# A hybrid decoder layer: sparse results stored as two halves, keys evacuated by whole tiles, one transpose for two heads' compressed probabilities

## The chip, the cores and the metric

The kernel runs on one core of a Trainium2 chip. A core has TensorE (PE in the profile; its weight loads are listed apart as PEld), VectorE (DVE), ScalarE (ACT), GpSimd (POOL) and SyncE (SP), which here issues all transfers of the kernel's data. The metric is the device time in microseconds of one execution; the median of three runs is compared.

## The reference

One layer on x of 1024 tokens by 1024 (float32). One input projection gives queries, keys and values of four differential-attention heads and of eight sparse (NSA) heads in two groups. An NSA head adds three gated attentions: over compressed keys (one per 32 tokens, stride 16, 63 in all), over selected blocks, and over a window of 512. All are concatenated, projected, added to the residual and normed; a SwiGLU feed-forward layer of width 2816 and a second norm follow. Cut to what the change touches:

```python
s_c = jnp.einsum('btghd,bngd->btghn', q, kc) * scale
p_cmp = masked_softmax(s_c, mask_c[None, :, None, None, :])
o_cmp = jnp.einsum('btghn,bngd->btghd', p_cmp.astype(dt), vc)
...
o = gates[..., 0:1] * o_cmp + gates[..., 1:2] * o_sel + gates[..., 2:3] * o_win
...
mix = jnp.concatenate([o_diff, o_nsa], axis=-1) @ w_out[l]
x = layer_norm(DEEPNORM_ALPHA * x + mix, ln1_g[l], ln1_b[l])
```

With 16 blocks of 64 keys and 16 chosen, all causal blocks are selected; the selected attention is a plain causal one.

## The kernel before, in words

**Precision by halves.** PE multiplies in fp32r. To keep float32's precision each operand is split into a rounded part "hi" and the rest "lo" (`split`, L79 to 83: a copy on ACT, then a subtraction on DVE or POOL), and a product is three matmuls, hi x hi, hi x lo and lo x hi (`mm3`, L114). Where the contraction is only 64 long, hi and lo are stacked in the 128 partitions instead. A key tile holds the 64 hi rows and the 64 lo rows of one head, a query tile holds the same 64 rows twice, and one matmul does the sum over both. In which half of the partitions hi lies makes no difference. Likewise a compressed value block (`vcc`) is stored twice, in the upper and the lower 64 partitions, and meets hi and lo of the compressed probabilities. In value tiles hi and lo stand side by side in the columns, so a result comes out as 128 partitions: 64 rows from hi and 64 from lo, which have to be added.

**Stages.** From 0 to 75 us the first projections; to about 410 the NSA units; to about 600 the differential-attention units; from about 500 to 660 the output projection with its norm; from 658 on the feed-forward layer, in a scheme with seven products for eight.

**NSA units** (`nsa_units`, L375). For each of four pairs of heads p and each of eight row blocks i there is a unit of kind 0 (compressed and selected) and one of kind 1 (window). `front` makes scores, exponentials and gated probabilities of both heads. `back` transposes the probabilities on PE (`transposed`, L361: transposes into a psT bank, copy, subtraction) and accumulates the results of both units in the one psO bank. A kind 0 unit begins with the compressed probabilities: two transposes of 128x64 into 64 partitions (L365), a copy of 64x256 (L371), a subtraction into the other 64 partitions (L372), one matmul (L418). A kind 1 unit ends with a copy of the lo rows (L433), an addition of the hi rows on DVE (L434) and two stores into `mix_d` (L436).

**Projections as fillers.** The projections of later keys, queries and values are "fillers" between the units: `phases` (L806) lists which units run with which fillers, and `pump` lets the fillers advance in step. `k_fill` (L525) projects one pair of key heads in two halves of 512 tokens into a psM bank. `evac_k` (L163) then copies the 64 rows of each head (L170) and puts the rest into the other 64 partitions of its tile (L171). Queries are moved between partitions by three transfers through SP (`move` in `evac_q`, L161).

**Output projection.** `out_start` (L589) loads x and the row block's mixed results, the NSA half of the columns first, then the differential half (`load_split_here`, L94, L99). It lands each in a `w` buffer (five in all) and splits it in place. `out_half` does 24 matmuls per half of the columns, NSA operands first. Rows 0 to 3 are fillers; rows 4 to 7 follow (L940 to 964).

**Order.** Each engine and SP's queue run their instructions in a fixed order. It is laid out when the kernel is built, by the priorities that the program gives (fillers get 2000 less urgent, L854) and a simulated timeline. An instruction that waits holds up all behind it on its engine; SP's transfers are such instructions.

Of the kernel before, what the change touches and what calls it, by code (L numbers as in the profile page):

```python
# [11 lines left out]
F32 = mybir.dt.float32  # L12
# [5 lines left out]
P = 128  # L18
# [19 lines left out]
def layer_kernel(ctx: ExitStack, tc: tile.TileContext, xT, x, w_t, w_vg, w_dv, lam_in, subln,  # L38
# [31 lines left out]

        return slots.tile([P, 1024], dt, tag="w", name="w", bufs=5)

    mix_d = dram.tile([NB, P, KT, P], F32, name="mix_d")
    wo_d = dram.tile([2, 4, P, 1024], F32, name="wo_d")
    x1_d = dram.tile([NB, P, DM], F32, name="x1_d")
    a_d = dram.tile([NF // 2, 7, P, 512], F32, name="a_d")
# [16 lines left out]

    def load_split_here(src, hi, lo, l_eng="dve", order=(0,)):  # L94

        n = 1024 // len(order)
        for k in order:
            raw = lo[:, k * n:(k + 1) * n].bitcast(F32)
            nc.sync.dma_start(raw, src[:, k * n:(k + 1) * n])  # L99
            split(raw, hi[:, k * n:(k + 1) * n], lo[:, k * n:(k + 1) * n], l_eng)  # L100
        return hi, lo
# [42 lines left out]
    with ExitStack() as ctx_a:  # L144
# [13 lines left out]
                    yield 0.33  # L158

        def move(dst, src):  # L160
            nc.sync.dma_start(dst.bitcast(F32), src.bitcast(F32))  # L161

        def evac_k(out):  # L163

            def f(hf, ps):
                cs = slice(hf * 512, (hf + 1) * 512)
                for g in range(2):
                    own = slice(g * 64, g * 64 + 64)
                    other = slice(64 - g * 64, 128 - g * 64)
                    nc.scalar.copy(out[g][own, cs], ps[own])  # L170
                    nc.vector.tensor_sub(out[g][other, cs], ps[own], out[g][own, cs].bitcast(F32))  # L171
            return f

        def evac_q(q, scale, ps):
# [183 lines left out]
            nc.scalar.copy(pt[:, :w], tp[:, :w])  # L358
            return pt

        def transposed(srcs, rows=P):  # L361

            tp = ps_t()
            for n, s in enumerate(srcs):
                nc.tensor.transpose(tp[:rows, n * P:(n + 1) * P], s, ident)  # L365
            w = len(srcs) * P
            pt = pt_tile().rearrange("p (h n) -> p h n", h=2)
            if rows == P:
                split(tp[:, :w], pt[:, 0, :w], pt[:, 1, :w])
            else:  # L370
                nc.scalar.copy(pt[0:rows, 0, :w], tp[0:rows, :w])  # L371
                nc.vector.tensor_sub(pt[rows:2 * rows, 0, :w], tp[0:rows, :w], pt[0:rows, 0, :w].bitcast(F32))  # L372
            return pt

        def nsa_units(p, qt, K, V):  # L375


            g = p // 2
            heads = (2 * p, 2 * p + 1)
            sl = [SLOPES[4 + h] for h in heads]  # L380
            state = {}

            def make(i, kind):
                nb = i + 1 if kind == 0 else min(i + 1, WIN_BLOCKS)
                j0 = i + 1 - nb
                width = nb * P
                ts = []

                def front():
                    dist = dsel[:, 1024 - width:] if kind == 0 else dwin[:, 640 - width:]  # L390
                    m = small([P, 4], "m", 4)
                    r = small([P, 4], "r", 4)
                    ts.extend(t_tiles(width))
                    if kind == 0:
                        pc = pa.tile([P, 2, NC], F32, tag="pc", name="pc", bufs=3)
                        ts.append(pc)
                    for a in range(2):
                        ms, rs = ([t[:, n:n + 1] for n in (a, 2 + a)] for t in (m, r))
                        cmp = (pc[:, a, :], dcmp[:, 56 - 8 * i:56 - 8 * i + NC], ms[1]) if kind == 0 else None
                        scores(q_of(qt, i, a), K[kind], j0 * P, width, dist, sl[a], ms[0], ts[a], cmp)  # L400
                        exps(ts[a], width, ms[0], rs[0])
                        if kind == 0:
                            exps(pc[:, a, :], NC, ms[1], rs[1])
                    nr = 2 if kind else 4
                    nc.vector.reciprocal(r[:, :nr], r[:, :nr])  # L405
                    for a in range(2):
                        for n, t in ((1 + kind, ts[a][:, :width]), (0, pc[:, a, :] if kind == 0 else None)):
                            if t is not None:
                                gc = heads[a] * 3 + n
                                c = a if n else 2 + a  # L410
                                nc.gpsimd.tensor_scalar(t, t, r[:, c:c + 1], gates[:, i, gc:gc + 1],  # L411
                                                        op0=ALU.mult, op1=ALU.mult)

                def back(fill):
                    if kind == 0:
                        state["po"] = po = ps_o()
                        ptc = transposed([ts[2][:, a, :] for a in range(2)], rows=64)
                        nc.tensor.matmul(po[:, :256], lhsT=vcc[g], rhs=ptc[:, 0, :256], start=True, stop=False)  # L418
                    po = state["po"]
                    for jj in range(0, nb, 2):  # L420
                        js = range(jj, min(jj + 2, nb))
                        pt = transposed([ts[a][:, j * P:(j + 1) * P] for j in js for a in range(2)])
                        for n, j in enumerate(js):
                            v = V[kind][:, (j0 + j) * P:(j0 + j + 1) * P]
                            last = kind == 1 and j == nb - 1
                            nc.tensor.matmul(po[:, :256], lhsT=v, rhs=pt[:, 0, n * 256:(n + 1) * 256],  # L426
                                             start=False, stop=False)
                            nc.tensor.matmul(po[:, :256], lhsT=v, rhs=pt[:, 1, n * 256:(n + 1) * 256],  # L428
                                             start=False, stop=last)
                        fill((jj + len(js)) / nb)  # L430
                    if kind == 1:
                        tmp = small([P, 256], "tmp", 3)[0:64, :]
                        nc.scalar.copy(tmp, po[64:128, :256])  # L433
                        nc.vector.tensor_add(tmp, po[0:64, :256], tmp)  # L434
                        for a in range(2):
                            nc.sync.dma_start(mix_d[i, a * 64:(a + 1) * 64, 4 + p, :], tmp[:, a * P:(a + 1) * P])  # L436

                return front, back, 2.0 * nb + 1

            return [make(i, kind) for i in range(NB) for kind in range(2)]  # L440
# [84 lines left out]
        def k_fill(n, where, out, halves=(0, 1)):  # L525
            def steps():
# [1 line left out]
                    out.extend([slot(m) for m in where])  # L528
                    out.append(load_split(w_t[n], *w_tiles(), l_eng="pool", pieces=2))
                for hf in halves:  # L530
                    yield from proj_steps(out[2], hf, evac_k(out))
                    there.add((n, hf))
            return steps, 5.2 * len(halves)

# [54 lines left out]
        def out_start(i):  # L589

            acc[i] = slot((8, 9, 10, 11, 4, 2, 3, 5)[i], F32)
            nc.sync.dma_start(acc[i], x[i * P:(i + 1) * P, :])
            mix_rows[i] = load_split_here(mix_d[i].rearrange("p k t -> p (k t)"), *w_tiles(),
                                           "dve" if i < 4 else "pool", order=(1, 0))

        def out_half(i, nh, ps):
            m = mix_rows[i]
# [673 lines left out]
```

## Time and profile before

| | us |
|---|---|
| median of three runs | 1304.74 (1304.59 to 1304.9) |
| the profiled execution | 1305.84 |
| its span, first to last instruction | 1304.1 |
| TensorE's mean granted clock | 0.999 |

How to read the profile: a group is named by line, engine, operation and tiles, "out<-in", with partitions x elements, its count, its busy time in us and the mean of one in ns, and then the engine's idle time just before it and what ended it. A line such as L83 is that of a helper, so the tile names tell the use. psS, psT, psO and psM are PSUM banks for scores, transposes, attention results and projections. Matmuls are pipelined and their records overlap, so a record's length isn't what the instruction costs in a stream. SPq is SP's queue.

### The profile page before, as it was taken

To read this page: it belongs to the slowest core of one execution; us is meant where nothing else is said; L and a number is where in the kernel's file an instruction comes from. 1 tells how busy PE (TensorE), PEld (TensorE's weight loads), DVE (VectorE), ACT (ScalarE), POOL (GpSimd) and SP (SyncE) were. 2 spreads that over 40 slices of the span, in tenths; PEclk is the share of its full clock that TensorE was granted. 3 is DMA by queue.
4 is the path that set the end of the run, shared out by engine and by line. 5 is a ranking of instruction groups with operands and counts; after the bars stand their busy time and mean duration, and the time that the engine had idled before them with its cause. 6 is when DMAs were issued, how large, how long until landed. Compare 5 with 4: busy or idle time off the path is not lost.

```text
span 1304.1 us, 20490 instructions
## 1 busy us (share of the span) xinstructions
PE 1286.2 (99%) x6955; PEld 1107.8 (85%) x6955; DVE 917.8 (70%) x1963; ACT 652.1 (50%) x1398; POOL 464.1 (36%) x499
## 2 busy tenths in 40 slices
PE   9999999999999999999999999999999999999997
PEld 7998999988988889788887888888888888888886
DVE  5567867778778667774797677776766768555588
ACT  5366866868776566653353333333333335533330
POOL 4434534545435446643613313232231222000071
PEclk9999999999999999999999999999999999999999
DMA  9412012121112135623224566555555559768641
GB/s 354 132 31 62 22 35 62 49 48 48 35 55 70 50 94 149 218 82 113 81 76 149 180 232 228 194 178 173 174 170 185 187 179 346 259 200 291 195 168 65
DMA packets 86841, 183.13 MB, mean 140 GB/s; under 512 B 10576, under 2 KB 19152, under 8 KB 86608
## 3 DMA queue, kind: packets, MB, share of 16 engines
q1 hardware_dynamic: 86736, 181.82, 42.7%
q8 instruction: 55, 0.90, 0.3%
q14 instruction: 50, 0.41, 0.1%
HBM read 116.18 MB, written 57.15 MB: 133 GB/s over the span
## 4 chain that ended last, share of the span: by engine, by line
PE 91%; DVE 4%; DMA 2%; ACT 2%; issue 1%; POOL 0%; SPq 0%; DVEq 0%; ACTq 0%
PE psM L116 11%; PE psM L118 11%; PE psM L117 11%; PE psS L118 6%; PE psS L117 6%; PE psS L116 6%; PE psT L118 5%; PE psT L117 5%; PE psT L116 5%; PE psT L365 4%; PE psS L323 3%; PE psS L326 3%; PE psO L428 2%; PE psO L426 2%; PE psO L481 2%; PE psO L116 2%
## 5 line engine op out<-in xcount | busy, mean ns | idle before, releaser
L346 ACT ACTIVATE t<-t,m 128x384 f32<-128x384 f32 (+7 forms) x192 | 144.2, 752 | 65.4 <-DVE m L332 59.8
L411 POOL TENSOR_SCALAR t<-t,r,gates 128x640 f32<-128x640 f32 (+7 forms) x128 | 99.6, 783 | 180.5 <-DVE r L405 82.4
L116 PE MATMUL psM<-big,w 128*128 128x512 f32 x304 | 120.6, 397 | 0.6 <-DVE slot L171 0.3
L118 PE MATMUL psM<-big,w 128*128 128x512 f32 x304 | 120.1, 396 | 0.0
L117 PE MATMUL psM<-big,w 128*128 128x512 f32 x304 | 119.9, 394 | 0.0
L323 PE MATMUL psS<-slot,q 128*128 128x320 f32 (+10 forms) x304 | 111.8, 369 | 2.2 <-DVE m L332 2.0
L1019 POOL TENSOR_TENSOR half<-half,half 128x512 f32<-128x512 f32 x22 | 33.5, 1524 | 205.0 <-ACT half L1018 205.0
L83 DVE TENSOR_TENSOR pt<-psT,pt 128x512 fp32r<-128x512 f32 (+1 forms) x152 | 91.3, 615 | 13.1 <-ACT pt L81 11.7
L326 PE MATMUL psS<-slot,q 128*128 128x320 f32 (+10 forms) x304 | 99.5, 329 | 0.0
L81 ACT CAST pt<-psT 128x512 fp32r<-128x512 f32 (+1 forms) x152 | 77.3, 525 | 20.6 <-PE psT L365 10.0
L81 ACT CAST big<-slot 128x1024 fp32r<-128x1024 f32 (+1 forms) x54 | 54.4, 1018 | 66.2 <-DVE slot L1011 50.5
L83 DVE TENSOR_TENSOR op<-op 128x1024 fp32r<-128x1024 f32 x44 | 60.9, 1388 | 36.3 <-ACT op L81 35.8
L83 DVE TENSOR_TENSOR big<-slot,big 128x1024 fp32r<-128x1024 f32 (+1 forms) x54 | 63.5, 1182 | 30.5 <-ACT big L81 30.3
L365 PE MATMUL psT<-ident,t 128*128 128x128 f32 x528 | 83.8, 273 | 0.8 <-DVE pt L83 0.7
L81 ACT CAST op<-op 128x1024 fp32r<-128x1024 f32 x44 | 45.9, 1052 | 61.8 <-DMA op<-t_d 55.6
L428 PE MATMUL psO<-pt,slot 128*128 128x256 f32 x264 | 72.1, 294 | 0.1
L426 PE MATMUL psO<-pt,slot 128*128 128x256 f32 x264 | 71.8, 289 | 0.0
L332 DVE CUSTOM_DVE_ANT_0 t<-psS,dsel 128x384 f32<-128x384 f32 (+9 forms) x128 | 62.3, 493 | 13.4 <-PE psS L326 9.6
L1023 POOL TENSOR_TENSOR half<-half,half 128x512 f32<-128x512 f32 x22 | 36.5, 1659 | 99.0 <-DVE half L1022 98.8
L81 ACT CAST big<-big 128x1024 fp32r<-128x1024 f32 (+1 forms) x49 | 44.2, 912 | 45.6 <-DMA big<-t_d 34.0
L118 PEld LDWEIGHTS psM<-big,w 128*128 128x128 f32 x304 | 57.1, 188 | 11.4
L116 PEld LDWEIGHTS psM<-big,w 128*128 128x128 f32 x304 | 57.2, 188 | 11.1 <-ACT w L81 0.8
(371 smaller groups left out, 3971.3 us busy)
## 6 DMA issues: line engine op xcount, KB each, us to landing
a_d<-slot SPq DMA_DIRECT2D x77, 256.0 KB, 3.0
t_d<-slot SPq DMA_DIRECT2D x77, 256.0 KB, 2.2
q<-q SPq DMA_DIRECT2D x48, 256.0 KB, 2.9
slot<-in_w_up_dram SPq DMA_DIRECT2D x22, 512.0 KB, 3.8
slot<-in_w_down_dram SPq DMA_DIRECT2D x22, 512.0 KB, 3.9
op<-a_d SPq DMA_DIRECT2D x44, 256.0 KB, 3.5
op<-t_d SPq DMA_DIRECT2D x44, 256.0 KB, 4.0
big<-a_d SPq DMA_DIRECT2D x33, 256.0 KB, 2.9
```

Source lines behind the costliest of these rows:

```text
L81: nc.scalar.copy(hi, src)
L83: eng.tensor_sub(lo, src, hi.bitcast(F32))
L116: nc.tensor.matmul(acc, lhsT=ah, rhs=bh, start=first, stop=False, skip_group_check=more)
L117: nc.tensor.matmul(acc, lhsT=ah, rhs=bl, start=False, stop=False, skip_group_check=more)
L118: nc.tensor.matmul(acc, lhsT=al, rhs=bh, start=False, stop=last, skip_group_check=more)
L323: mm = nc.tensor.matmul(ps[:, :c + part], lhsT=q[0], rhs=k[:, ks], start=True, stop=False)
L326: nc.tensor.matmul(ps[:, :c + part], lhsT=q[1], rhs=k[:, ks], start=False, stop=True)
L346: nc.scalar.activation(t[:, :width], t[:, :width], AF.Exp, bias=m, scale=-1.0, accum_out=r)
L365: nc.tensor.transpose(tp[:rows, n * P:(n + 1) * P], s, ident)
L411: nc.gpsimd.tensor_scalar(t, t, r[:, c:c + 1], gates[:, i, gc:gc + 1], op0=ALU.mult, op1=ALU.mult)
L426: nc.tensor.matmul(po[:, :256], lhsT=v, rhs=pt[:, 0, n * 256:(n + 1) * 256], start=False, stop=False)
L428: nc.tensor.matmul(po[:, :256], lhsT=v, rhs=pt[:, 1, n * 256:(n + 1) * 256], start=False, stop=last)
```

## The change

Three edits.

1. `back` of a kind 0 unit calls the new `transposed_cmp`: one transpose of both heads' probabilities together (128 columns, so head a comes out in partitions 64a to 64a+63), then for each head a copy of 64x128 and a subtraction of 64x128 into the other partitions. The old special case for 64 rows goes from `transposed`.
2. `back` of a kind 1 unit copies all 128 partitions of psO and stores hi and lo rows apart, in `mixs_d`, by two transfers; the addition on DVE falls away. `out_start` loads both halves, adds them on POOL in a third `w` buffer, splits the sum, and then loads the differential half from `mix_d`, which has become half as wide.
3. `k_fill` evacuates with the new `evac_k_whole`: one copy of 128x512 into the first tile, one subtraction of 128x512 into the second, and then three transfers that swap the upper half of the second tile with the lower half of the first, by way of a piece of DRAM, `turn_d`. The first key projection keeps `evac_k`.

```diff
-    mix_d = dram.tile([NB, P, KT, P], F32, name="mix_d")
+    mix_d = dram.tile([NB, P, 4, P], F32, name="mix_d")
+    mixs_d = dram.tile([NB, 2, P, 4, P], F32, name="mixs_d")
+    turn_d = dram.tile([5, 2, 64, 512], F32, name="turn_d")
...
+        def evac_k_whole(out, n):
+
+            def f(hf, ps):
+                cs = slice(hf * 512, (hf + 1) * 512)
+                nc.scalar.copy(out[0][:, cs], ps)
+                nc.vector.tensor_sub(out[1][:, cs], ps, out[0][:, cs].bitcast(F32))
+                up, down = out[1][0:64, cs], out[0][64:128, cs]
+                move(turn_d[n, hf], down)
+                move(down, up)
+                move(up, turn_d[n, hf])
+            return f
...
+        def transposed_cmp(pc):
+
+            tp = ps_t()
+            nc.tensor.transpose(tp[:, :P], pc.rearrange("p a n -> p (a n)"), ident)
+            pt = pt_tile()[:, :2 * P]
+            for a in range(2):
+                own, other = slice(a * NC, (a + 1) * NC), slice((1 - a) * NC, (2 - a) * NC)
+                cs = slice(a * P, (a + 1) * P)
+                nc.scalar.copy(pt[own, cs], tp[own, :P])
+                nc.vector.tensor_sub(pt[other, cs], tp[own, :P], pt[own, cs].bitcast(F32))
             return pt
...
-                        ptc = transposed([ts[2][:, a, :] for a in range(2)], rows=64)
-                        nc.tensor.matmul(po[:, :256], lhsT=vcc[g], rhs=ptc[:, 0, :256], start=True, stop=False)
+                        nc.tensor.matmul(po[:, :256], lhsT=vcc[g], rhs=transposed_cmp(ts[2]), start=True, stop=False)
...
                     if kind == 1:
-                        tmp = small([P, 256], "tmp", 3)[0:64, :]
-                        nc.scalar.copy(tmp, po[64:128, :256])
-                        nc.vector.tensor_add(tmp, po[0:64, :256], tmp)
-                        for a in range(2):
-                            nc.sync.dma_start(mix_d[i, a * 64:(a + 1) * 64, 4 + p, :], tmp[:, a * P:(a + 1) * P])
+                        tmp = small([P, 256], "tmp", 3)
+                        nc.scalar.copy(tmp, po[:, :256])
+                        for n in range(2):
+                            nc.sync.dma_start(mixs_d[i, n, :, p, :].rearrange("(a e) t -> e a t", a=2),
+                                              tmp[n * 64:(n + 1) * 64, :].rearrange("e (a t) -> e a t", a=2))
...
-                    yield from proj_steps(out[2], hf, evac_k(out))
+                    yield from proj_steps(out[2], hf, evac_k_whole(out, (n - 9) // 2 if n > 3 else 4))
...
-            mix_rows[i] = load_split_here(mix_d[i].rearrange("p k t -> p (k t)"), *w_tiles(),
-                                           "dve" if i < 4 else "pool", order=(1, 0))
+            raw, m, l_eng = w_tile(F32), w_tiles(), "dve" if i < 4 else "pool"
+            parts = [raw[:, n * 512:(n + 1) * 512] for n in range(2)]
+            for n in range(2):
+                nc.sync.dma_start(parts[n], mixs_d[i, n].rearrange("p k t -> p (k t)"))
+            nc.gpsimd.tensor_add(parts[0], parts[0], parts[1])
+            split(parts[0], m[0][:, 512:1024], m[1][:, 512:1024], l_eng)
+            load_split_here(mix_d[i].rearrange("p k t -> p (k t)"), m[0][:, 0:512], m[1][:, 0:512], l_eng)
+            mix_rows[i] = m
```

More of the change, by code (lines that the diff above doesn't have):

```diff
@@ L94, in load_split_here @@
     def load_split_here(src, hi, lo, l_eng="dve", order=(0,)):
-        n = 1024 // len(order)
+        n = src.shape[-1] // len(order)
         for k in order:
@@ L160, in move @@
         def move(dst, src):
-            nc.sync.dma_start(dst.bitcast(F32), src.bitcast(F32))
+            nc.sync.dma_start(*(t if t.dtype == F32 else t.bitcast(F32) for t in (dst, src)))
         def evac_k(out):
@@ L359, in transposed_whole, with transposed @@
             return pt
-        def transposed(srcs, rows=P):
+        def transposed(srcs):
             tp = ps_t()
             for n, s in enumerate(srcs):
-                nc.tensor.transpose(tp[:rows, n * P:(n + 1) * P], s, ident)
+                nc.tensor.transpose(tp[:, n * P:(n + 1) * P], s, ident)
             w = len(srcs) * P
             pt = pt_tile().rearrange("p (h n) -> p h n", h=2)
[L368 to L372, printed above, removed]
+            split(tp[:, :w], pt[:, 0, :w], pt[:, 1, :w])
+            return pt
+        def transposed_cmp(pc):
[7 more added lines that the diff above has]
+                nc.vector.tensor_sub(pt[other, cs], tp[own, :P], pt[own, cs].bitcast(F32))
             return pt
```

## The prediction

> **What bounds the kernel now.** I read the page first, then the busy time by stretch, then what TensorE waited for, then single rows of the timeline.
>
> ```profile
> span 1304.1 us, 20490 instructions
> PE 1286.2 (99%) x6955; PEld 1107.8 (85%) x6955; DVE 917.8 (70%) x1963; ACT 652.1 (50%) x1398; POOL 464.1 (36%) x499
> PE 91%; DVE 4%; DMA 2%; ACT 2%; issue 1%; POOL 0%; SPq 0%; DVEq 0%; ACTq 0%
> ```
>
> TensorE (PE) is busy for 99% of the span and carries 91% of the chain that ended last. So two things only can move the time: the number and length of PE's instructions, and the few places where PE waits. The stretches show where those are:
>
> ```profile
> 0.00:75.00 75.00, 72.24 (x399) 62.61 (x400) 40.41 (x97) 35.50 (x81) 32.07 (x64) 1.00 0.61 212
> 75.00:410.00 335.00, 331.20 (x2258) 302.99 (x2257) 251.67 (x889) 248.09 (x679) 150.81 (x215) 1.00 0.19 47
> 410.00:480.00 70.00, 70.00 (x430) 62.42 (x429) 44.45 (x130) 38.91 (x104) 31.98 (x34) 1.00 0.22 58
> 480.00:550.00 70.00, 67.21 (x438) 59.46 (x437) 49.74 (x148) 47.62 (x129) 45.73 (x47) 1.00 0.61 180
> 550.00:700.00 150.00, 148.54 (x776) 124.79 (x775) 108.33 (x189) 64.65 (x125) 57.67 (x46) 1.00 0.27 92
> 700.00:1304.00 604.00, 597.00 (x2665) 495.57 (x2664) 423.24 (x511) 217.29 (x284) 145.81 (x95) 1.00 0.59 200
> ```
>
> The columns after the stretch's length are the busy us of PE, PE's weight loads, VectorE (DVE), ScalarE (ACT) and GpSimd (POOL). The change touches the sparse (NSA) attention, which lies in 75 to 410, the key projections up to 485, and the output projection, in 500 to 660. There PE is idle for 335.00 - 331.20 = 3.80, 0, 2.79 and 1.46 us. From 700 on PE is idle only behind its last product, and nothing there is edited: what is won before it reaches the end undiminished.
>
> Now the length of a transpose. Its record is not its price, since records overlap:
>
> ```profile
> L365 PE MATMUL psT<-ident,pc 128*64 128x128 f32 x64 | 14.6, 272 | 0.0
> ...
> 221.31 0.27 PE L365 MATMUL psT<-ident,pc 128*64 128x128 f32 x1
> 221.34 0.36 PE L428 MATMUL psO<-pt,slot 128*128 128x256 f32 x1
> 221.54 0.28 PE L426 MATMUL psO<-pt,slot 128*128 128x256 f32 x1
> 221.66 0.28 PE L428 MATMUL psO<-pt,slot 128*128 128x256 f32 x1
> ```
>
> The compressed transpose starts at 221.31 and the second product behind it at 221.54. One product of 256 columns takes 221.66 - 221.54 = 0.12 us from start to start, so the transpose put 0.23 - 0.12 = 0.11 us into PE's stream, though its record lasts 0.272.
>
> **Part by part.** *One transpose for both heads.* The 64 transposes of 64 columns become 32 of 128. The moving operand is the identity, 128 columns in both, so each costs the same: 32 x 0.11 = 3.5 us less on PE, all on the path. The row bounds it at 0.11 per transpose, since no idle time stands at this line. Behind it, one copy and one subtraction of 64x256 become two of 64x128 each:
>
> ```profile
> L371 ACT CAST pt<-psT 64x256 fp32r<-64x256 f32 x32 | 11.5, 359 | 3.9 <-PE psT L365 3.2 <-PE psO L418 0.3
> L372 DVE TENSOR_TENSOR pt<-psT,pt 64x256 fp32r<-64x256 f32 x32 | 13.3, 417 | 2.4 <-ACT pt L371 1.5
> L358 ACT COPY pt<-psT 128x128 f32<-128x128 f32 x8 | 2.1, 263 | 0.7 <-PE psO L481 0.5
> L485 DVE COPY od<-psO 128x128 f32<-128x128 f32 x32 | 9.2, 288 | 16.9 <-PE psO L481 16.6
> ```
>
> At the 128-column rows, ACT goes from 0.359 to 2 x 0.263, which is 32 x 0.167 = 5.3 us more; DVE from 0.417 to 2 x 0.288, 32 x 0.159 = 5.1 us more. From transpose to product the wait grows from 0.359 + 0.417 = 0.78 to 0.263 x 2 + 0.288 = 0.81, the second copy lying beside the first subtraction. The other blocks' products cover that; uncovered it is 32 x 0.03 = 1.0. I take +0.2.
>
> *The sparse results.* ACT's copy goes from 64x256 to 128x256, the addition on DVE falls away:
>
> ```profile
> L433 ACT COPY tmp<-psO 64x256 f32<-64x256 f32 x32 | 11.8, 369 | 8.8 <-PE psO L428 8.1
> L434 DVE TENSOR_TENSOR tmp<-psO,tmp 64x256 f32<-64x256 f32 x32 | 13.1, 410 | 8.7 <-ACT tmp L433 8.4
> L81 ACT CAST pt<-psT 128x256 fp32r<-128x256 f32 x40 | 14.6, 368 | 4.6 <-PE psO L418 2.7 <-PE psT L365 1.5
> ...
> PE psO L481 <- DVE tmp L434: 0.8, 1, 0.8
> ```
>
> A copy of 128 partitions lasts as long (368) as one of 64 (369), so ACT pays nothing. DVE loses 32 x 0.41 = 13.1 us, and the one psO bank comes free 0.41 earlier. PE ever waited for that addition once, 0.8 us. I take -0.4, within 0 and -0.8. The two stores per unit move 64 KB each instead of 32; nobody waits for them before the output projection.
>
> *Keys by whole tiles.* Five projections by two halves are ten evacuations. Each had two copies and two subtractions; it keeps one of each, and adds three dependent transfers of 128 KB on SP:
>
> ```profile
> L170 ACT CAST slot<-psM 64x512 fp32r<-64x512 f32 x20 | 11.5, 580 | 2.9 <-DVE slot L171 1.8 <-PE psM L118 0.6 <-PE psS L326 0.4
> L171 DVE TENSOR_TENSOR slot<-psM,slot 64x512 fp32r<-64x512 f32 x20 | 13.8, 689 | 1.4 <-ACT slot L170 0.8
> 281.10 0.69 DVE slot L171
> ...
> 281.81 0.70 DVE pt L83
> 282.65 0.63 PE L365 MATMUL psT<-ident,t 128*128 128x128 f32 x4 [0.71 <-DVE pt L83]
> 370.56 0.70 DVE slot L171
> 480.75 0.68 DVE slot L171
> mix_d<-tmp SPq DMA_DIRECT2D x16, 128.0 KB, 2.8
> SPq L161 <- DMA q<-q: 35.8, 17, 5.2
> ```
>
> That takes 10 x 0.69 = 6.9 us from DVE and 10 x 0.58 = 5.8 from ACT. The 281 rows show what one is worth: PE idled 0.71 us for a subtraction of probabilities that stood on DVE right behind a key's. The chain runs through this line also at 370.56 and 480.75. I take 0.33 for each of the three places, -1.0; the ends are 0 and the whole 6.9. A key is whole some 3 x 2.8 = 8.4 us later than before. Cover: by the order of the fills a key half is followed by at least one more fill or unit before its first reader, and its two last halves in a phase are read a phase later. On SP, the second and third move wait for the one before, as the query moves do now (2.1 us each on average, 35.8 / 17); behind them in SP's queue stand the next weights and the sparse stores. If all that cover were gone, ten halves x 2 x 2.1 = 42 us of SP would be blocked, but PE would notice only where it runs out of weights. I take 0, with up to +2 (one such wait).
>
> *The output rows.* Each of eight rows loads two halves instead of one, adds them on POOL, and takes three w buffers of the five instead of two, one only until the cast and subtraction:
>
> ```profile
> L1019 POOL TENSOR_TENSOR half<-half,half 128x512 f32<-128x512 f32 x22 | 33.5, 1524 | 205.0 <-ACT half L1018 205.0
> w<-mix_d SPq DMA_DIRECT2D x16, 256.0 KB, 2.8
> ```
>
> At the row of the same size POOL pays 8 x 1.52 = 12 us, and has 150.00 - 57.67 free in the stretch where most of it falls. A row is ready about 1.5 + 0.4 us later. Its sparse half doesn't depend on late work and can be fetched early. I take +0.3; the ends are 0 and the rival's 7 below.
>
> Sum: -3.5 + 0.2 - 0.4 - 1.0 + 0.3 = -4.4 us. DVE sheds 13.1 + 6.9 - 5.1 = 14.9 us, but PE was short of DVE so seldom that only 1.4 of that is counted. The profiled execution took 1305.84 (span 1304.1 and 1.74 around it), 1.10 above the median of 1304.74; its own time becomes 1301.4, and a median 1300.3.
>
> **The rivals.** (1) *No change.* The pace of 75 to 410 is set not by PE's stream but by DVE and ACT (251.67 and 248.09 of 335 busy), so PE waits through what the transposes leave. For it: DVE stands on 4% of the chain, and these waits of PE name DVE:
>
> ```profile
> PE psS L323 <- DVE m L332: 2.0, 4, 0.8
> PE psT L365 <- DVE pt L83: 0.7, 1, 0.7
> ```
>
> Against it: PE idles for 3.80 us there, and DVE sheds work too. The same result comes if the instructions, whose order is laid out anew when the kernel is built, happen to cost PE some 3 more us of waits, as many as 480 to 550 now has (2.79). Either way the 3.5 is eaten: 1303.7, give or take 1.5.
>
> (2) *Slower: the last output row waits for its buffers.* Row 7 can't take all its w buffers until row 5 is done with them:
>
> ```profile
> 634.61 0.39 PE L118 MATMUL psM<-big,w 128*128 128x512 f32 x1
> 634.85 1.14 ACT L81 CAST w<-w 128x512 fp32r<-128x512 f32 x2 [2.14 <-issue]
> 646.66 0.39 PE L116 MATMUL psM<-big,w 128*128 128x512 f32 x1
> L647 POOL TENSOR_TENSOR slot<-slot,slot 128x1024 f32<-128x1024 f32 x11 | 27.3, 2484 | 12.1 <-ACT slot L646 12.1
> SPq L609 <- DVE slot L648: 43.6, 6, 11.1
> ```
>
> Row 5's last product starts at 634.61, row 7's casts at 634.85, its first product at 646.66: 11.8 us of cover. If the landing buffer too comes free only there, the loads (2.8 + 0.4), the addition (1.5) and the cast (0.57) take 5.3, and PE sees nothing. But if those loads queue on SP behind the store of a normed row (up to 11.1 us of waiting) and the addition behind a layer norm's multiply (2.5), it is 18.9, and PE idles 7.1. It decides as soon as that queueing is over 11.8 - 5.3 = 6.5 us. Then -4.4 + 7.1 = +2.7: 1307.4. Against it: the loads can be put ahead of the store in SP's order, and transposes of other rows can fill PE.
>
> (3) *A transpose costs what its record says*: 32 x 0.272 = 8.7 instead of 3.5, so -9.6 and 1295.1. The Trainium skill, "TensorE: Matmul & The Clock Gate", Part 4 (PE-mode transpose), puts a 128x128 transpose at about 275 ns in a kernel's context, most of it access latency. This trace's record agrees with that length (272) and not with it as a price: the start-to-start of 0.11 decides, which leaves the rival little.
>
> **The numbers.** Forecast 0.60, rival 1 0.23, rival 2 0.13, rival 3 0.04. Over 0.2% (2.6 us, about what a measurement of this kernel can tell from no change) lie the forecast and rival 3: faster 0.64, same 0.23, slower 0.13. The time is the forecast's, 1300.3. The range runs from 1297.0 (1304.74 - 3.5, less half of the key term's 6.9 and psO's 0.8, with nothing lost elsewhere) to 1306.0 (rival 1 with the 2 us of SP); rival 3, most of rival 2 and thin tails stay out, some 2 in 10.
>
> **What would show it.** Right: 32 transposes less at the pc line and PE's busy time about 3.5 us down by start-to-start; DVE's busy time down by some 15, with the new subtractions near 0.29; PE idle in 75 to 410 not above 3.8; everything from 700 on unchanged, moved up as a block. Rival 1: PE idle in 75 to 550 up by 3 or more. Rival 2: PE waiting for a w cast, or a POOL addition, near 640. Wrong: a product of scores waiting for a key's move, or a pair of 64x128 instructions far above 0.26 and 0.29.

## The result, and the profile after

The changed kernel takes 1318.13 us in the median of four runs (1315.94 to 1321.95), the kernel before 1304.73 in the same series: ratio 1.0102, 95% interval 1.0082 to 1.0122. It is slower; the forecast was 1300.3. The profiled execution took 1321.95.

From the page of the kernel after:

```profile
span 1320.0 us, 20480 instructions
PE 1289.8 (98%) x6923; PEld 1109.6 (84%) x6923; DVE 914.7 (69%) x1953; ACT 648.9 (49%) x1420; POOL 476.5 (36%) x507
PE 85%; DVE 6%; DMA 3%; issue 2%; ACT 2%; POOL 1%; DVEq 0%; SPq 0%; ACTq 0%; POOLq 0%
```

PE has its 32 products less (6923 for 6955), yet it is idle for 1320.0 - 1289.8 = 30.2 us where it was idle for 17.9: 12.3 more. Its busy time is 3.6 up instead of 3.5 down, 7.1 too much. The mean granted clock is 0.994 for 0.999, and 0.005 x 1320 = 6.6 us. So the 15.9 us of span are 12.3 of waits and 7.1 of slower products, less the 3.5 forecast for the products saved. DVE, DMA, ACT and POOL carry 12% of the chain that ended last, 8% before.

The stretches of the kernel after (columns as before: PE, PE's loads, DVE, ACT, POOL, granted clock):

```profile
75.00:410.00 335.00, 330.32 (x2248) 302.26 (x2247) 243.72 (x891) 248.96 (x710) 152.15 (x217) 1.00 0.25 62
480.00:550.00 70.00, 61.60 (x371) 54.14 (x370) 40.60 (x117) 39.20 (x108) 43.23 (x43) 0.95 0.60 181
550.00:700.00 150.00, 143.66 (x760) 120.67 (x759) 108.36 (x196) 62.79 (x124) 67.14 (x54) 0.99 0.30 101
700.00:1304.00 604.00, 603.33 (x2664) 498.73 (x2663) 429.14 (x512) 224.77 (x297) 147.14 (x95) 1.00 0.59 199
```

The sparse stage is nearly as tight as before (4.68 us idle for 3.80). The loss stands behind it: 8.40 idle for 2.79 in 480 to 550, 6.34 for 1.46 in 550 to 700, and there the clock is below 1. From 700 to 1304 PE is idle for 0.67 us; what it idles behind its last product (7.00 us in this stretch before) lies past 1304 here. PE's waits in the whole kernel after (engine, tile and line, the instruction waited for: us in all, times, longest):

```profile
PE psT L521 <- DVE od L518: 5.8, 2, 3.2
PE psS L337 <- DVE m L346: 4.0, 10, 0.7
...
PE psT L940 <- DVE xT3l L85: 1.7, 1, 1.7
PE psT L521 <- DVE r L485: 1.7, 1, 1.7
```

The largest is the last step of a differential-attention unit, where `od` waits for its norm. Follow the first of its two waits upstream, GpSimd's row first:

```profile
503.76 0.49 POOL L490 TENSOR_TENSOR t<-t 128x144 f32<-128x144 f32 x1
508.74 1.29 POOL L618 TENSOR_TENSOR w<-w 128x512 f32<-128x512 f32 x1 [4.48 <-DMA w<-mixs_d]
510.01 0.76 POOL L489 TENSOR_SCALAR t<-t,r 128x192 f32<-128x192 f32 x1
510.74 1.03 POOL L517 TENSOR_TENSOR ss<-ss,mhalf 128x4 f32<-128x4 f32 x1
```

then VectorE's, and TensorE's:

```profile
511.80 1.08 DVE L518 TENSOR_TENSOR od<-od,ss 128x512 f32<-128x512 f32 x1 [3.43 <-POOL ss L517]
```
```profile
510.06 0.28 PE L119 MATMUL psM<-slot,big 128*128 128x256 f32 x1
513.02 0.83 PE L521 MATMUL psT<-ident,od 128*128 128x128 f32 x4 [2.69 <-DVE od L518]
```

The new addition of a row's halves (L618) sits on GpSimd for 4.48 us until its load has landed. Behind it in the queue stand a softmax step (L489) and the norm's power (L517). DVE's `od` waits for the power, and PE for `od`: it issues nothing from 510.06 to 513.02, and is idle for 2.69 us of that. What the hole leaves behind is in the kernel after's stretches of 2 us:

```profile
513.00:515.00 2.00, 1.98 (x10) 1.85 (x11) 1.20 (x6) 0.60 (x2) 0.87 (x3) 0.58 0.00 0
515.00:517.00 2.00, 2.00 (x12) 2.00 (x11) 0.73 (x4) 1.71 (x6) 0.56 (x2) 0.57 0.00 0
517.00:519.00 2.00, 2.00 (x16) 1.78 (x15) 1.00 (x5) 1.75 (x6) 0.00 (x0) 1.00 0.45 131
```

PE is busy, but for 4 us at 0.57 of its clock, which is 1.7 us more lost. The kernel before had no such hole and a clock of 1.00 there.

The groups that the change touched, in the kernel after:

```profile
L388 PE MATMUL psT<-ident,pc 128*128 128x128 f32 x32 | 8.7, 273 | 0.0
L393 ACT CAST pt<-psT 64x128 fp32r<-64x128 f32 x64 | 16.5, 257 | 6.9 <-PE psT L388 4.4 <-DVE pt L394 1.3 <-PE psO L439 0.2
L394 DVE TENSOR_TENSOR pt<-psT,pt 64x128 fp32r<-64x128 f32 x64 | 18.5, 288 | 6.7 <-ACT pt L393 4.7
L181 DVE TENSOR_TENSOR slot<-psM,slot 128x512 fp32r<-128x512 f32 x10 | 6.8, 687 | 0.8 <-ACT slot L180 0.8
L618 POOL TENSOR_TENSOR w<-w 128x512 f32<-128x512 f32 x8 | 11.9, 1492 | 8.7 <-DMA w<-mixs_d 5.3 <-ACT slot L673 2.6 <-PE psT L369 0.8
```

Every duration is as forecast: DVE's edited groups sum to -13.8 - 13.3 - 13.1 + 6.8 + 18.5 = -14.9. One entry is new, a ScalarE copy (L393) that waits for a VectorE subtraction (L394), 1.3 us in all. One unit of it, on ScalarE and on VectorE:

```profile
222.40 0.24 ACT L393 CAST pt<-psT 64x128 fp32r<-64x128 f32 x1
...
224.72 0.26 ACT L393 CAST pt<-psT 64x128 fp32r<-64x128 f32 x1
```
```profile
223.19 0.28 DVE L394 TENSOR_TENSOR pt<-psT,pt 64x128 fp32r<-64x128 f32 x1
...
225.92 0.29 DVE L394 TENSOR_TENSOR pt<-psT,pt 64x128 fp32r<-64x128 f32 x1
```

Copy, subtraction, copy, subtraction, each begun after the one before, as the program writes them, with other work of both engines between. From first copy to last subtraction it is 3.8 us (226.21 - 222.40). This unit is one of the longer ones: the mean of the 32 is 2.85 us (1.45 to 4.62). In the kernel before, the one copy and the one subtraction took 1.23 us in the mean (0.80 to 2.22), with other work between there too. In all 32 units the second copy begins only after the first subtraction has ended. In this sequence TensorE hardly notices: the listed waits for L394 hold only one of its weight loads, for 0.3 us.

### The profile page after: what moved, and what is told of

Read it like the earlier page. It is cut to its first block, busy times and chain, and to the rows that moved or that the text cites. A ratio compares the mean times of both kernels' runs of the same rounds, so it can differ in the third digit from the quotient of the medians.

```text
span 1320.0 us, 20480 instructions
## 1 busy us (share of the span) xinstructions
PE 1289.8 (98%) x6923; PEld 1109.6 (84%) x6923; DVE 914.7 (69%) x1953; ACT 648.9 (49%) x1420; POOL 476.5 (36%) x507
## 4 chain that ended last, share of the span: by engine, by line
PE 85%; DVE 6%; DMA 3%; issue 2%; ACT 2%; POOL 1%; DVEq 0%; SPq 0%; ACTq 0%; POOLq 0%
PE psM L118 10%; PE psM L119 10%; PE psM L120 10%; PE psS L118 5%; PE psS L119 5%; PE psS L120 5%; PE psT L120 5%; PE psT L119 5%; PE psT L118 5%; PE psT L379 4%; PE psS L337 3%; PE psS L340 3%; PE psO L449 2%; PE psO L447 2%; PE psO L502 2%
## 5 line engine op out<-in xcount | busy, mean ns | idle before, releaser
L1046 POOL TENSOR_TENSOR half<-half,half 128x512 f32<-128x512 f32 x22 | 33.5, 1525 | 202.7 <-ACT half L1045 202.7
L85 DVE TENSOR_TENSOR pt<-psT,pt 128x512 fp32r<-128x512 f32 (+1 forms) x152 | 91.7, 616 | 16.6 <-ACT pt L83 15.8
L85 DVE TENSOR_TENSOR op<-op 128x1024 fp32r<-128x1024 f32 x44 | 60.5, 1385 | 41.4 <-ACT op L83 40.8
L85 DVE TENSOR_TENSOR big<-slot,big 128x1024 fp32r<-128x1024 f32 (+1 forms) x54 | 64.8, 1205 | 29.7 <-ACT big L83 29.5
L379 PE MATMUL psT<-ident,t 128*128 128x128 f32 x528 | 82.2, 273 | 1.8 <-DVE pt L85 1.0
L337 PEld LDWEIGHTS psS<-slot,q 128*128 128x128 f32 x304 | 58.0, 191 | 13.6 <-DVE m L346 7.8
L379 PEld LDWEIGHTS psT<-ident,t 128*128 128x128 f32 x528 | 62.1, 140 | 6.0 <-issue 2.0
L120 PEld LDWEIGHTS psM<-big,w 128*128 128x128 f32 x304 | 57.3, 188 | 11.4
```

The lines of the kernel that those rows point to most:

```text
L85: eng.tensor_sub(lo, src, hi.bitcast(F32))
L120: nc.tensor.matmul(acc, lhsT=al, rhs=bh, start=False, stop=last, skip_group_check=more)
L337: mm = nc.tensor.matmul(ps[:, :c + part], lhsT=q[0], rhs=k[:, ks], start=True, stop=False)
L379: nc.tensor.transpose(tp[:, n * P:(n + 1) * P], s, ident)
```

## The experiments

Eighteen kernels, each timed beside the kernel before (1305.1 to 1305.4 in these series). "Own" is the sequence that the build lays out for a kernel; "of ..." is another kernel's, in which its instructions are held.

| work | sequence | us | ratio, 95% interval |
|---|---|---|---|
| keys alone | own | 1303.16 | 0.9986 [0.9977, 0.9995] |
| transposes alone | own | 1313.2 | 1.0063 [1.0051, 1.0076] |
| output rows alone | own | 1313.9 | 1.0061 [1.0049, 1.0074] |
| keys and transposes | own | 1313.89 | 1.0072 [1.0059, 1.0085] |
| transposes, copies grouped | own | 1311.87 | 1.0048 [1.0035, 1.006] |
| the same | of before, product early | 1313.44 | 1.0065 [1.0052, 1.0078] |
| the same | of before, product late | 1307.23 | 1.0019 [1.001, 1.0028] |
| one wide pair behind the product | of before, product late | 1301.64 | 0.9974 [0.9965, 0.9982] |
| before | of the grouped transposes | 1310.44 | 1.0037 [1.0025, 1.005] |
| before, heads in the other sequence | own | 1305.52 | 1.0002 [0.9993, 1.0011] |
| output rows alone | of before | 1307.1 | 1.0018 [1.0009, 1.0027] |
| before | of the rows alone | 1318.87 | 1.0104 [1.009, 1.0118] |
| keys alone | of before | 1314.07 | 1.0068 [1.0056, 1.0081] |
| whole change | of before | 1324.56 | 1.015 [1.0136, 1.0164] |
| before | of the kernel after | 1338.74 | 1.0256 [1.0242, 1.027] |
| after, no GpSimd addition | of after | 1312.49 | 1.0057 [1.0044, 1.0069] |
| the same, one wide pair | of after | 1314.4 | 1.007 [1.0056, 1.0083] |
| keys, grouped transposes late | of the keys alone | 1305.18 | 0.9999 [0.999, 1.0008] |

**One part at a time.** Theory: the output rows' loads and addition hold GpSimd's queue. Rivals: the keys' moves block SyncE; or any edit is laid out anew and loses by that. The edits are the change's own hunks:

```diff
# only_keys
+                    yield from proj_steps(out[2], hf, evac_k_whole(out, (n - 9) // 2 if n > 3 else 4))
# only_transposes
+                        nc.tensor.matmul(po[:, :256], lhsT=vcc[g], rhs=transposed_cmp(ts[2]), start=True, stop=False)
# only_rows
+            nc.gpsimd.tensor_add(parts[0], parts[0], parts[1])
# no_rows: the first two
```

> The kernel before with the whole-tile evacuation of the keys alone. Theory (output rows): within 2 us of 1304.7, rather below. Rival K (keys' moves): most of the loss is here, 1313 or more, with PE waiting for weights or keys between 75 and 550. Rival O (order alone): anywhere, 5 us or more from 1304.7.

> The kernel before with the one transpose for both heads alone. Theory (the output rows' extra load, their addition on POOL and what waits behind it cost the time): 32 x 0.11 = 3.5 us less on PE and nothing else of weight, 1301.2, within 1300 to 1303. Rival K (the keys' moves block SP's queue): the same. Rival O (any edit makes a new order at build, and the order alone costs the time): not 1301 but 5 us or more away from it.

> The kernel before with the sparse halves stored apart and added on POOL in the output rows alone. Theory (output rows): the loss is here, 1304.7 + 13 to 18, so 1317 to 1322, with PE idle in 500 to 560 and after 650 as in the changed kernel. Rival K (keys' moves): within 3 us of 1304.7. Rival O (order alone): anywhere.

> The changed kernel without the stored halves: transposes and keys as changed, results added on DVE and stored whole as before. Theory (output rows): 1304.7 - 3.5 - 0 to 1 = 1300 to 1302. Rival K (keys' moves): 1313 or more. Rival O (order alone): neither, and not the sum of the two single edits.

The keys win 1.9 us. Rows and transposes lose 8 to 9 each, and the two parts that don't touch the output rows lose as much together as all that the rows lose alone. So the theory cannot be the whole, and the numbers do not add.

**Work against sequence.** The build orders every engine's instructions anew for each kernel. To part the two, a kernel's instructions were tied to the order of another (a real dependency comes first where it speaks against it). The kernel before was not held in its own sequence, so the price of the tie itself was not measured; that it is small is seen from held kernels that took 1301.64 and 1305.18:

```diff
+    for a, b in zip(order, order[1:]):
+        tc.add_manual_dep(traced[b], traced[a].name,
+                          mybir.DependencyInfo(mybir.DependencyClass.NoSync, mybir.DependencyReason.DATA),
+                          reason="order")
```

and, in the grouped kernels, the alternation of copy and subtraction was taken out:

```diff
-            for a in range(2):
-                own, other = slice(a * NC, (a + 1) * NC), slice((1 - a) * NC, (2 - a) * NC)
-                cs = slice(a * P, (a + 1) * P)
-                nc.scalar.copy(pt[own, cs], tp[own, :P])
-                nc.vector.tensor_sub(pt[other, cs], tp[own, :P], pt[own, cs].bitcast(F32))
+            for own, other, cs in parts:
+                nc.scalar.copy(pt[own, cs], tp[own, :P])
+            for own, other, cs in parts:
+                nc.vector.tensor_sub(pt[other, cs], tp[own, :P], pt[own, cs].bitcast(F32))
```

> The changed transposes alone, as in the run of that part, but with both copies of the turned probabilities written ahead of both subtractions, so that the second copy no longer waits for the first subtraction. Theory W (the ping-pong of ScalarE and VectorE, copy-subtraction-copy-subtraction, holds the weighted sums back and costs the 6.8 us between the predicted -3.5 and the +3.3 that stood at the end of the sparse stage; the loss at 503 to 560 us follows from it): the sparse stage ends near 404 us and the kernel takes 1301 to 1304 us. Theory O (the instructions of every engine are laid out anew when the kernel is built, for the durations that the builder assumes, and the new layout costs more waits than the products save): the layout is new here too, 1034 of TensorE's 6736 products stand elsewhere, so anything from 1301 to 1318, and near the 1313 of the ungrouped edit more likely than below 1303.

> The same work as transposes_grouped, with every engine's instructions held in the sequence that the kernel before has (the one product in the place of the first of the two it replaces, the pairs of copies and subtractions in the place of the single ones). Theory O: with the old layout the 3.5 us show: 1300.5 to 1303, and it is well below transposes_grouped. Theory W: the same time as transposes_grouped within 1.5 us. A third case, that the pairs of narrow copies and subtractions themselves hold TensorE up: no gain, 1304 or more, in both.

> The kernel before, its work untouched, with every engine's instructions held in the sequence of transposes_grouped. Theory O: it loses what transposes_grouped loses, that is the time of transposes_grouped plus 1 to 4 us, above 1307 if transposes_grouped is above 1304. Theory W: 1304.7 to 1306, whatever transposes_grouped takes.

In `heads_reversed` nothing is tied; only the two loops over the heads in `front` of a sparse unit are turned round:

```diff
-                    for a in range(2):
+                    for a in (1, 0):
```

> The kernel before with the two heads of each unit of the sparse stage taken in the other sequence; the work is the same, only the layout of the instructions comes out anew (262 of TensorE's products stand elsewhere). Theory O: the time leaves 1304.7 by more than 2 us, to either side, and the place is 503 to 560 us if it is slower. Theory W: 1304.7 within 1 us.

Both theories fall in their pure form. The new sequence alone costs the unchanged work 5.3 us. But the new work in the old sequence costs 8.3, more than in its own, and one new sequence (heads reversed) costs nothing. The third case on record, that the narrow pairs themselves hold TensorE up, had forecast no gain in both sequences, and none came. What the work lost in the old sequence is one line among PE's waits in 75 to 410 of `grouped_old_order`:

```profile
PE psT L374 <- POOL pc L420: 7.0, 7, 1.5
```

The product needs the probabilities of both heads. In the place of the first of the two old ones it waits for GpSimd to finish the second head.

**Rows and the whole, held.**

> The change of the sparse results and output rows alone (1313.9 us in the layout that it gets when built), with every engine's instructions held in the sequence of the kernel before: all 6768 products and all 1108 ScalarE instructions stand as before, the 8 additions on GpSimd just ahead of the copies that need them. The runs of the transposes left two causes standing side by side: the new sequence alone cost 5.3 us there, and the new work in the old sequence 8.3. Theory O (the sequence costs it): 1303 to 1306. Theory W (the second row load and the addition on GpSimd hold the softmax's steps behind them, the cause that the prediction's second rival named for the output rows): 1309 to 1315, with TensorE's holes between 503 and 560 us.

> The kernel before, its work untouched, in the sequence that the run of the rows alone had (all 6768 products in that sequence). Theory O: 1309 to 1314. Theory W: 1304 to 1307.

> The whole change, every engine's instructions held in the sequence of the kernel before; the one product of 128 columns stands in the place of the second of the two that it replaces, not of the first (in the run with the grouped copies it stood in the place of the first, and TensorE waited 7.0 us for the second head's probabilities there). Theory O: the products' 3.5 us and the keys' 1.6 to 2.7 are left, less some waits for the copies that alternate with the subtractions: 1299 to 1305. Theory W: 1309 to 1318.

> The kernel before, its work untouched, in the sequence of the kernel after (6704 of its 6736 products in that sequence, and each second transpose beside its first). Theory O: it loses most of what the kernel after lost in spite of its saved products: 1312 to 1322. Theory W: 1304 to 1307.

For the rows the sequence is the larger part: their work loses 8.8 us in its own and 1.9 in the old one (1307.1, between the ranges of the two theories). The unchanged work loses 13.7 in theirs (1318.87, more than the 1314 that the theory of the sequence allowed). In `before_rows_order` PE idles 9.08 us in 75 to 410, 5.3 more than in the kernel before:

```profile
75.00:410.00 335.00, 325.92 (x2205) 296.19 (x2204) 243.34 (x864) 242.50 (x663) 147.24 (x210) 1.00 0.18 46
```

and its waits in 480 to 560 begin with

```profile
PE psS L323 <- DMA q<-q: 2.4, 1, 2.4
```

scores that wait for a query's move. The whole change loses 19.4 in the old sequence, which the theory of the sequence had put at 1299 to 1305: it misses there. Among PE's waits in `after_old_order` stand

```profile
PE psT L369 <- ACT pt L372: 7.7, 1, 7.7
PE psO L439 <- DVE pt L394: 4.0, 4, 1.5
...
PE psT L379 <- DVE pt L394: 1.1, 2, 0.7
```

Here TensorE does wait for the alternating narrow subtractions (L394), 5.1 us in all; the 7.7 are followed up below. And a sequence fits the work it was laid out for: the 33.6 us that the unchanged work loses in the sequence of the kernel after are no measure of what that sequence costs the kernel after.

**What costs in the old sequence.** In `grouped_late` the product stands where the second of the two old ones stood. In `one_pair` the narrow pairs behind it are one wide pair (so the second head's compressed probabilities reach no columns of their own):

```diff
-            for own, other, cs in parts:
-                nc.scalar.copy(pt[own, cs], tp[own, :P])
-            for own, other, cs in parts:
-                nc.vector.tensor_sub(pt[other, cs], tp[own, :P], pt[own, cs].bitcast(F32))
+            nc.scalar.copy(pt[:, :P], tp[:, :P])
+            nc.vector.tensor_sub(pt[:, P:2 * P], tp[:, :P], pt[:, :P].bitcast(F32))
```

> The transposes alone with both copies ahead of both subtractions, in the sequence of the kernel before, as grouped_old_order, but the one product of 128 columns stands in the place of the second of the two products that it replaces. Theory J (the join: one product needs the probabilities of both heads, and standing in the first one's place it waited 7.0 us for the second head's in seven places): TensorE's waits for pc fall from 7.0 to under 2 us, the sparse stage ends 3 to 6 us earlier than the 414.1 there, and the kernel takes 1303 to 1309. Theory P (the pairs of narrow copies and subtractions behind the product are what holds TensorE): 1311 to 1314 as before, with the waits now at the weighted sums' first product.

> As grouped_late, but with one copy and one subtraction of 128 partitions by 128 columns behind the product in place of the two narrow pairs; the second head's compressed probabilities are not put into columns of their own, so that the compressed sums lose their meaning, while products, waits and everything else stand. Theory P: 3 us or more below grouped_late, and below the 1305.2 of the kernel before by up to the 3.5 us that the products save: 1301 to 1304. Theory J alone: within 1.5 us of grouped_late.

> The keys' part alone (1303.2 in its own layout), in the sequence of the kernel before: all products stand as before, the three moves of each half where its subtraction stood. In after_old_order the last keys' second move was issued at 495.4 and the third at 497.6, the eight loads of the output weights behind them at 499.3 to 503, and TensorE then had one hole of 7.7 us at 501 to 509 behind ScalarE's cast of these weights. Theory S (each further move through memory blocks SyncE's queue for the 2 us of the move ahead, and the weights behind it come late): the same hole here, 4 us or more, 1307 to 1312. If the hole came from the sparse results' stores or the row loads of the other parts: no hole, 1302 to 1305.

The join: 1313.44 - 1307.23 = 6.2 us, gone with the late place; the idle time at the transpose is 0.1 there for 7.0:

```profile
L374 PE MATMUL psT<-ident,pc 128*128 128x128 f32 x32 | 8.8, 274 | 0.1
```

The narrow pairs, two for one wide one: 1307.23 - 1301.64 = 5.6 us. By which waits they cost it is open: those listed for their `pt` in `grouped_late` are 0.8 us, and the kept trace of `one_pair` is its slowest run (1304.59). With the wide pair the kernel is 1305.4 - 1301.64 = 3.8 us faster than before, about the 3.5 that the products should save. That is not the products alone, as the wide pair (0.257 + 0.284 us) is also shorter than the pair before (0.359 + 0.417). Their price shows directly in the kernel after: behind 11 of the 32 transposes at L388 stands another transpose, and each time it starts 0.11 us later. Both theories were right, each for its part.

The keys, which win in their own sequence, lose 8.7 in the old one (1314.07; 1307 to 1312 was forecast for the hole). SyncE's queue in `keys_old_order` (second column: until the last of a group is issued):

```profile
480.37 0.46 SPq L162 DMA_DIRECT2D slot<-slot  x1
482.61 0.46 SPq L162 DMA_DIRECT2D slot<-turn_d  x1
483.18 0.53 SPq L100 DMA_DIRECT2D w<-mix_d  x1
483.75 0.46 SPq L162 DMA_DIRECT2D turn_d<-slot  x1
486.69 0.46 SPq L162 DMA_DIRECT2D slot<-slot  x1
488.89 0.46 SPq L162 DMA_DIRECT2D slot<-turn_d  x1
489.44 1.05 SPq L518 DMA_DIRECT2D mix_d<-tmp  x2
490.54 0.48 SPq L100 DMA_DIRECT2D big<-wo_d  x1
```

and in the kernel before:

```profile
484.62 7.90 SPq L99 DMA_DIRECT2D big<-wo_d  x8
```

A move waits some 2.2 us for the one ahead (480.37 to 482.61, 486.69 to 488.89), and the output weights queue behind six of them (the first at 474.66): issued at 490.54 for 484.62. ScalarE's cast waits for them, everything behind it on ScalarE waits too, and then PE, in the same kernel:

```profile
493.50 0.62 ACT L82 CAST big<-big 128x512 fp32r<-128x512 f32 x1 [10.45 <-DMA big<-wo_d]
```
```profile
500.23 0.48 PE L368 MATMUL psT<-ident,t 128*128 128x128 f32 x1 [7.12 <-ACT pt L371]
```
```profile
500.00:502.00 2.00, 1.77 (x8) 1.69 (x9) 1.23 (x6) 2.00 (x7) 1.81 (x4) 0.50 0.01 4
502.00:504.00 2.00, 2.00 (x10) 2.00 (x10) 1.50 (x4) 2.00 (x7) 1.96 (x3) 0.50 0.00 0
504.00:506.00 2.00, 2.00 (x10) 1.66 (x9) 2.00 (x5) 1.07 (x3) 2.00 (x3) 0.63 0.88 186
```

A hole of 7.1 us, then half the clock for some 5. It is the hole of 7.7 that the whole change had in the old sequence. In their own sequence (`only_keys`) the first output weight is issued at 481.85, between two moves, and there is no such hole.

**In the kernel after's own sequence.** The eight additions are taken out, the sequence held; one half of the sparse results is left out so. In the second kernel the narrow pairs are one wide pair as well.

```diff
-            nc.gpsimd.tensor_add(parts[0], parts[0], parts[1])
```

> The kernel after in its own sequence, held, without the eight GpSimd additions of the sparse results' halves (the first half alone is used, so the output lacks the other); all loads and all other instructions stand. Theory G (the first of these additions waits 4.5 us for its second load on GpSimd and holds the softmax's steps behind it, which is TensorE's hole of 2.85 us at 510 us and the lower clock behind it): the hole is gone, 1312 to 1315. Rival (the split of the same tile waits for the same load on other engines, or the next wait comes in its place): 1317 to 1319.

> The kernel after in its own sequence, without the eight GpSimd additions, as after_no_addition (1312.5), and with one copy and one subtraction of 128 by 128 behind the product of 128 columns in place of the two alternating narrow pairs (so the compressed sums and one half of the sparse results are left out). Theory P (the narrow pairs hold TensorE, 5.6 us between grouped_late and one_pair in the old sequence): 1305 to 1309. Rival (the new sequence sets the pace, the pairs lie beside other waits in it): 1311 to 1313.

Without the additions it takes 1312.49, 5.6 us less. GpSimd's softmax step and power come 7 us earlier in `after_no_addition`,

```profile
502.94 1.05 POOL L489 TENSOR_SCALAR t<-t,r 128x192 f32<-128x192 f32 x1 [1.73 <-DVE ss L516]
503.95 1.02 POOL L517 TENSOR_TENSOR ss<-ss,mhalf 128x4 f32<-128x4 f32 x1
```

and 505 to 515, where the kernel after had the hole, is full at full clock:

```profile
505.00:515.00 10.00, 10.00 (x82) 9.74 (x82) 6.22 (x22) 6.78 (x22) 3.37 (x7) 1.00 0.54 162
```

So the eight additions are shown as a cause, worth 5.6 of the 13.4. The trace puts most of it on the head-of-line wait at the first row, 2.69 of idle time and 1.7 of slower clock; the rest isn't parted. The wide pair brings nothing there (1314.4, if anything slower; PE now waits 4.7 us for `pt` at L379 in 75 to 410, where it waited 1.0). That in a sequence laid out for the narrow pairs their time is other work's room would explain it, but is not shown.

That leaves 7 us over the kernel before that no single edit was shown to carry. Most of it lies in waits and a lower clock between 525 and 560 of `after_no_addition`: PE idles 6.8 us there (2.7 in the kernel before), and the clock is 0.50 from 534 to 538. The longest wait is the second of the two for `od`. Among PE's waits in `after_no_addition`, and in `before_after_order` where the work is unchanged, stand

```profile
PE psT L521 <- DVE od L518: 3.2, 1, 3.2
```
```profile
PE psT L500 <- DVE od L497: 3.2, 1, 3.2
...
PE psT L500 <- DVE r L464: 1.7, 1, 1.7
```

The 3.2, and the 1.7 that the kernel after also had, come with the sequence and not with the changed work. In `after_no_addition` VectorE's sum for this norm (L516, at 529.02) stands behind the subtraction of a `w` tile (L85, 526.26), before which VectorE idled 3.27 us; in the kernel before, the same norm's power was done at 525.10, and PE's list has no wait for `od`. Why the build lays the changed work out with them, and whether a sequence exists in which all three parts win, stays open.

**A faster version?**

> The keys' part and the transposes with grouped copies, the sparse results as in the kernel before, in the sequence that the keys alone got (1303.2), the product of 128 columns in the place of the second of the two. If the parts add where the sequence is held: 1303.2 plus the 1.8 us of grouped_late, 1304 to 1306. If the keys' shorter evacuation leaves VectorE and ScalarE room for the narrow pairs: 1300 to 1303, and it beats both kernels.

The parts add, in a held sequence: what the transposes lose eats what the keys win. The one version below both kernels that leaves no work out is the keys alone, 1303.16 (0.9986 [0.9977, 0.9995]), 15 us under the whole change.

## Why the prediction was wrong

- *The products, -3.5.* Right in its mechanism, and the size fits: 0.11 us from start to start again, and 3.8 in `one_pair`, its shorter pair included. Rival 3, the record's length (8.7), fits neither.
- *The evacuation behind the transpose, +0.2, "the second copy lying beside the first subtraction".* This step failed. The second copy never lay beside the first subtraction, and the pairs take 2.85 us in the mean where 0.81 stood; the old pair took 1.23 and not 0.78, since other work lies between. TensorE waits 5.1 us for these subtractions in `after_old_order`, though only 0.3 in the kernel after's own sequence. Even grouped, the narrow pairs cost 5.6 us in the old sequence where "the other blocks' products cover that" stood. The prediction also did not see that one product joins two heads; with the product in the wrong place that costs 6.2.
- *Sparse results, -0.4, and output rows, +0.3 with 7 at the far end.* Both together are +1.9 in the old sequence. In the sequence of the kernel after, the eight additions alone are 5.6. Rival 2 had the right queue, GpSimd's and SyncE's, but the wrong place: the prediction looked at row 7 near 640, where PE does not wait, and not at the first rows, whose loads land while the differential units need GpSimd. That POOL has 150.00 - 57.67 us free was no answer: what counts is what stands behind the waiting instruction.
- *Keys, -1.0 with 0 to +2 for SyncE.* In their own sequence -1.9, inside the bounds. In the old one +8.7: the bound of one wait of 2.1 us was too small, since six moves stood ahead of the output weights.
- *The waits of before carried over.* This is the step that turned the sign. The sum took PE's 17.9 us of idle time as given and subtracted from it; the sequence is laid out anew, and the idle time came out at 30.2. Rival 1 named this ("laid out anew") with some 3 us, and its sign came: PE's idle time in 75 to 550 is up by 6.5. Measured on unchanged work in new sequences the loss is 0.3 (heads reversed), 5.3 and 13.7. A term of that spread should have set the range, on the slow side above all, for a kernel whose sequence is already tight can mostly lose.
- *The clock.* Not in the sum at all: 6.6 us.
- *Right:* DVE -14.9 in the edited groups, and the block from 700 on, which takes about as long as before (619.2 us from the first L1046 to the end, 618.1 from L1019 before). But DVE's whole busy time fell by 3.1 only (917.8 to 914.7), where "down by some 15" stood: groups that nobody edited grew, `od` at L518 from 6.9 to 9.9 us.

## What to carry to other kernels

Price an edit by what queues behind it: where a new instruction waits on an in-order engine or queue (an addition for a load, a move for a move), list what stands behind it and who waits for that. Merging two products saved their cycles here but added a join, and the narrow pairs behind them ate the saving. Where a build lays out the sequence, test an edit in the old sequence and the old work in the new one before believing a sum of a few microseconds.

## What was not expected of the hardware

An idle time of 2.69 us on PE (before 513.02) was followed by 4 us at a granted clock of 0.57 to 0.58, one of 7.12 us by 6 us at 0.50 to 0.63. One of 2.38 us (before 514.78 in `before_rows_order`) was followed by 0.50 from 516 to 518. So a hole costs more than its length: 2.7 us more in the second case (2 x 0.50 + 2 x 0.50 + 2 x 0.37). The Trainium skill, "TensorE: Matmul & The Clock Gate", Part 1 (The HAM clock gate), says that an idle array drops to half its rate and that the first 3.4 us of work run so. The traces agree with the half rate and with some microseconds of it; the section's warning against idle gaps above about 3.4 us is not the safe side here, where 2.69 and 2.38 were enough.
